# A two-batch encoder layer: eight places for the split operands of the seven block products, later stores of y, uneven output steps per attention round, and 30 steps ahead of the mixture

## Chip, core and metric

The kernel runs on one core of one Trainium2 chip. Its time is the device time of one execution in microseconds; several runs are shown and their median is compared. Beside them stands one execution under the hardware profiler, from which all durations here are read.

## What is computed

One hybrid encoder layer runs on two token sets with the same weights: A (`x_prompt`, 1024 tokens) and B (`x_sample`, 512 tokens), 1024 channels, all in float32.

```python
h = rms_norm(x, pre_w)
cols = jnp.einsum('bsd,dc->bsc', h, w_in)
y_m = mlstm_mixer(...) * jax.nn.silu(m_z)          # 1024 wide
y_a = dilated_attention(a_qkv, rel_table) * jax.nn.silu(a_z)   # 3 groups x 8 heads x 64
p_m = jnp.einsum('bsc,cd->bsd', y_m, w_pm)
p_a = jnp.einsum('bsc,cd->bsd', y_a, w_pa)
merged = g[:, :, 0] * p_m + g[:, :, 1] * p_a
out = jnp.einsum('bsd,de->bse', merged, w_out)
return x + rms_norm(out, post_w)
```

The three dilation groups of the attention are mixed with weights made of their row maxima and softmax denominators ("the mixture").

## The kernel before

**Arithmetic.** Float32 products are made of rounded halves: every operand is split into a high part (ScalarE copy) and a low part (VectorE subtraction), and `mm3` (L233 to L235) issues three matmuls: high x high, high x low, low x high. One such triple on 128x512 is one *step* of the filling work. The large products of A's output side (`w_proj_m` and `w_out` on 1024 x 1024 x 1024 pieces) are made with seven block products in place of eight (i = 0 to 6): sums and differences of the operand quadrants are formed on GpSimd (L2248), split into *places* by `divide` (L2233 and L2234), multiplied, and added up by VectorE when a PSUM bank is evicted.

**Order of the work.** TensorE and the SP queue run in the program's order; the other engines' instructions are placed by the framework's scheduler. `Fill` holds the filling work as a list of generators that give one step at a time. The mixers (mLSTM, attention, the mixture) are the foreground: after each of their rounds they call `fill(share)`, and `fill.stage(steps, shares)` sets how many steps a share is worth. When B's attention begins (L2877), 768 steps are done. What then follows, in steps: the last four input units (32); for A the projection `proj_m` in seven block products of 16 (112), `proj_a` (64) and `final`, the output product with the closing norm, again seven of 16 (112); then B's branches: `proj_m` (64), `proj_a` (32), and B's `final` (64). 1248 steps in all.

**B's attention** (`attend`, L1926) runs 12 heads' pairs x 4 tiles = 48 rounds and three closing ones. In the last 16 rounds (group 2, `compact`) four rounds form a batch: scores (`lg`, L1719), maxima and exponents (L1730, L1732 on VectorE, L1734 on ScalarE), two transposes (`pt`, L1742), and the output product (`o`, L1751). `STEPS[3] = 290` steps are spread over the 48 rounds, 6.04 each.

**The mixture** (`combine`, L2032) follows for B's four token tiles t. It loads the rows `og_b` that attention has stored (`V0a`, `V1a`), forms weights on VectorE (`weigh`, L2052 to L2062), scales (`mix`, L2069), adds (L2075), transposes on TensorE (`tp`, L2080) and multiplies with the gate (L2082). Its first load is issued at the first `next(mixed)`; two shares of filling follow before the first `weigh`, of 66/18 steps each times two.

**A's `final`** (L2391). Its operands a0, b0, a1, b1 are the four merged quadrants. `combined` (L2237) lists the splits and sums as jobs; a job that reuses a place is held until the last step that read it. The places are a ring: `V0b`, `V1b` and `H0` in `proj_m`, `V0b`, `V1b` and `K1` in `final`, two places each, so six. The evictions are L2431 to L2447: `u` (`H1`), `o` (`H2`), `x` (`H0`) hold running sums. When a token tile is complete, `square` sums squares on ScalarE (L2414) and multiplies with the norm's weight on GpSimd (L2415), and `close` adds it to the residual on VectorE (L2424) and queues the store of y. Queued stores of y go to the SP queue at the next eviction in `final` (`flush`), or after two ticks.

**B's `proj_m`** needs the eight rows `yb` of B's mLSTM output, split by `split` (L2152; L2167 on ScalarE, L2168 on VectorE) while the last 26 steps of `final` run: into `X0`, `K0` (rows 0 to 3) and `H3`, `H2` (rows 4 to 7). They come through three row buffers (`ymr`, `sraw`), whose loads stand in GpSimd's queue.

Of the kernel before, what the change touches and what calls it, by code (L numbers as in the profile page):

```python
# [29 lines left out]
P = 128  # L30
# [174 lines left out]
class Net:  # L205
# [1720 lines left out]
    def attend(self, T, fill, steps, first, banks, outs, after=None, beside=None, at=()):  # L1926
# [5 lines left out]
        with ExitStack() as st:  # L1932
# [269 lines left out]
    def outputs(self, T, before):  # L2202
# [34 lines left out]
        def combined(kind, ring, uses, begun):  # L2237
# [46 lines left out]
        def proj_m(weights):  # L2284
            ring = M["ring"] + slots("H0")
            M["a1"], M["b1"] = four("H1"), four("H2")
            quadrant(M["b1"], 4, 1)
            quadrant(M["a1"], 0, 1)
            for n in range(2):
                gate(n)  # L2290
            u, x = four("H3"), four("Q1")
            pm = M["pm"] = {(0, 0): four("X0"), (0, 1): u, (1, 1): x}
            uses = [(i, k) for i in range(7) for _ in range(4) for k in range(4)]
# [10 lines left out]
            def evict(i, p, ps):  # L2304
                q, r = u[:, p], x[:, p]
                if i == 0:
                    nc.scalar.activation(q, ps, AF.Copy)
                elif i in (1, 4):
                    if (i, p) == (4, 0):
                        pm[1, 0] = four("K0")  # L2310
                    y = pm[i // 4, 0][:, p]
# [21 lines left out]
            def halves(b, k):  # L2333
                if k == 0:
                    ya.append([four(z, F32R) for z in (("K1", "H1"), ("H2", "H0"))[b]])
# [4 lines left out]
            for b, t in ((0, 82), (1, 97)):  # L2340
                late += [(t + k, lambda b=b, k=k: row(b, k)) for k in range(3)]
# [49 lines left out]
        def final(weights):  # L2391
            fill, sb = weights.__self__, self.osb
            ring = M["ring"] + slots("K1")
            u, o, x = four("H1"), four("H2"), four("H0")
            tiles = [(i, t) for i in range(7) for t in range(4)]
# [21 lines left out]
            def close(b, t, ys):  # L2417
# [5 lines left out]
                for h, y in enumerate(ys):  # L2423
                    nc.vector.scalar_tensor_tensor(xt[h], y, s[:, 6:7], xt[h], op0=OP.mult, op1=OP.add)  # L2424
                    self.pending.append((self.clock + 2, "y", (T.y[r0:r0 + P, h * S:(h + 1) * S], xt[h]), ("xo", which)))

            def evict(i, t, ps):
                q, r = u[:, t], x[:, t]
                self.flush(lambda q: q[1] == "y")
                if i == 0:  # L2430
# [54 lines left out]
            assert not jobs  # L2485
            self.flush(lambda q: q[3] == ("xo", "gab"))
            self.xo_bufs = [q for q in self.xo_bufs if q[0] != "gab"]
            self.retired = self.spare_place
            free = len(self.wsplit) - (len(fill.ready) - fill.base)
            places = [self.take(z) for z in ("Q1", "H0")]  # L2490
            self.wsplit[free:free] = [[z[:, 1024 * i:1024 * (i + 1)] for i in range(2)] for z in places]
# [139 lines left out]
SHORT = 768  # L2631
STEPS = (316, 260, 192, 290, 66)


def body(tc, a):
# [3 lines left out]
    with ExitStack() as st:  # L2639
# [158 lines left out]
        with ExitStack() as s1:  # L2798
# [82 lines left out]
            with ExitStack() as s2:  # L2881
# [80 lines left out]
```

## Time and profile before

| what | value |
| --- | --- |
| time of the runs shown | 2222.4, 2214.58, 2217.93 us; median 2217.93 us |
| the profiled execution's own time | 2215.37 us |
| its span, first to last instruction | 2213.6 us |
| mean granted TensorE clock | 0.989 |
| TensorE matmuls | 2168.8 us busy, 98% of the span, 11530 instructions |
| VectorE | 1531.7 us, 69% |
| ScalarE | 1093.1 us, 49% |
| GpSimd | 850.5 us, 38% |
| DMA | 408.22 MB, mean 184 GB/s |

A row of the profile reads: line of the kernel, engine, operation, output tile <- input tiles, shape, count; then busy time and mean duration, then idle time of that engine just before, and what ended it. In a timeline the first two numbers are the start and the duration in us, and the bracket holds the idle time ahead. Matmuls overlap in the pipeline, so their starts tell the pace, not their durations. PEclk is the granted TensorE clock, 1.00 for full speed.

### The profile page before, as it was taken

How to read it: one execution, taken by the hardware profiler on the slowest of the kernel's cores; microseconds unless marked ns; L12 is line 12 of the kernel's file. 1: busy time of each engine (PE TensorE's matmuls, PEld its weight loads, DVE VectorE, ACT ScalarE, POOL GpSimd, SP SyncE). 2: the span in 40 equal slices, each digit the busy share in tenths (PEclk: the TensorE clock that was granted, in tenths of full speed). 3: DMA queues.
4: the chain of work that ended last, by engine and by line, in shares of the span. 5: the costliest groups of instructions: out<-in, count | busy, mean ns of one | idle time of the engine just before them, and what ended most of it. 6: DMA issues, size and time to landing. Idle time of an engine off the chain costs nothing. (4 is left out here: it accounts for less than half of the span.)

```text
span 2213.6 us, 33670 instructions
## 1 busy us (share of the span) xinstructions
PE 2168.8 (98%) x11530; PEld 1847.1 (83%) x11530; DVE 1531.7 (69%) x2967; ACT 1093.1 (49%) x2252; POOL 850.5 (38%) x1077
## 2 busy tenths in 40 slices
PE   9999999999999999999999999999999999999598
PEld 8988888888888888888888889998888878877487
DVE  8766565667778776548887765665578748857774
ACT  7322243344444433447776666666655545436322
POOL 1000432333335663236677630011155443475531
PEclk9999999999999999999999999999999999999799
DMA  3642454723335553386755658977687785745763
GB/s 137 191 137 79 149 163 143 220 105 114 105 114 179 181 197 134 118 271 216 237 166 179 194 176 240 280 205 199 210 279 260 243 285 155 233 136 173 257 203 112
DMA packets 213430, 408.22 MB, mean 184 GB/s; under 512 B 36905, under 2 KB 118505, under 8 KB 213258
## 3 DMA queue, kind: packets, MB, share of 16 engines
q1 hardware_dynamic: 184104, 298.17, 42.3%
q0 software_dynamic: 25552, 95.30, 13.4%
q10 hardware_dynamic: 3602, 12.59, 1.4%
q8 instruction: 91, 1.49, 0.3%
q14 instruction: 81, 0.66, 0.1%
HBM read 278.91 MB, written 127.07 MB: 183 GB/s over the span
## 5 line engine op out<-in xcount | busy, mean ns | idle before, releaser
L234 PE MATMUL dense<-H,wh 128*128 128x512 f32 x700 | 276.2, 395 | 5.8 <-DVE H L2168 5.8
L233 PE MATMUL dense<-H,wh 128*128 128x512 f32 x660 | 270.0, 409 | 11.7 <-ACT H L2167 11.7
L235 PE MATMUL dense<-H,wl 128*128 128x512 f32 x660 | 260.2, 394 | 0.0
L233 PE MATMUL d<-Hh,phla 128*128 128x512 f32 x608 | 236.5, 389 | 0.0
L235 PE MATMUL d<-Hh,phla 128*128 128x512 f32 x608 | 236.5, 389 | 0.0
L234 PE MATMUL d<-Hl,phla 128*128 128x512 f32 x608 | 236.5, 389 | 0.0
L302 DVE TENSOR_TENSOR wl<-wraw,wh 128x1024 fp32r<-128x1024 f32 (+1 forms) x122 | 153.9, 1263 | 41.1 <-ACT wh L296 40.8
L235 PE MATMUL d<-Hh,phlb 128*128 128x512 f32 x456 | 177.4, 389 | 0.0
L233 PE MATMUL d<-Hh,phlb 128*128 128x512 f32 x456 | 177.4, 389 | 0.0
L234 PE MATMUL d<-Hl,phlb 128*128 128x512 f32 x456 | 177.4, 389 | 0.0
L296 ACT ACTIVATE wh<-wraw 128x1024 fp32r<-128x1024 f32 (+1 forms) x125 | 129.3, 1036 | 61.7 <-PE dense L234 33.7
L234 PEld LDWEIGHTS dense<-H,wh 128*128 128x128 f32 x700 | 133.0, 190 | 22.7 <-DVE H L2168 6.7
L782 POOL TENSOR_TENSOR psum_w<-pw_raw 128x512 f32<-128x512 f32 x38 | 59.5, 1565 | 236.1 <-DMA pw_raw<-w_in 154.3
L233 PEld LDWEIGHTS dense<-H,wh 128*128 128x128 f32 x660 | 125.2, 190 | 29.1 <-ACT H L2167 12.9
L235 PEld LDWEIGHTS dense<-H,wl 128*128 128x128 f32 x660 | 124.8, 189 | 28.1
L1839 DVE CUSTOM_DVE_ANT_0 ls<-lg,bias 128x256 f32<-128x256 f32 (+2 forms) x240 | 78.7, 350 | 89.7 <-PE lg L1820 51.8
L234 PEld LDWEIGHTS d<-Hl,phla 128*128 128x128 f32 x608 | 114.1, 188 | 23.7
L233 PEld LDWEIGHTS d<-Hh,phla 128*128 128x128 f32 x608 | 114.1, 188 | 23.7
L819 POOL TENSOR_TENSOR psum_w<-pw_raw,psum_w 128x512 f32<-128x512 f32 x38 | 49.3, 1298 | 220.1 <-DVE phla L764 220.1
L235 PEld LDWEIGHTS d<-Hh,phla 128*128 128x128 f32 x608 | 114.1, 188 | 23.7
L1843 ACT ACTIVATE ls<-ls,nm 128x256 f32<-128x256 f32 (+1 forms) x192 | 87.3, 456 | 80.0 <-DVE nm L1841 49.2
L233 PE MATMUL d<-v,Hh 128*128 128x484 f32 (+1 forms) x336 | 121.3, 361 | 0.1
(780 smaller groups left out, 6011.7 us busy)
## 6 DMA issues: line engine op xcount, KB each, us to landing
pw_raw<-w_in SPq DMA_DIRECT2D x76, 512.0 KB, 3.8
wraw<-w_in SPq DMA_DIRECT2D x63, 512.0 KB, 4.7
aqk_a<-pwk SPq DMA_DIRECT2D x32, 512.0 KB, 7.1
Q<-aqk_a SPq DMA_DIRECT2D x20, 512.0 KB, 6.3
wraw<-w_v POOLq DMA_DIRECT2D x22, 430.0 KB, 6.2
aqk_b<-sw SPq DMA_DIRECT2D x36, 256.0 KB, 6.5
aqk_a<-pwk SPq DMA_DIRECT2D x32, 256.0 KB, 3.8
qk_a<-pwk SPq DMA_DIRECT2D x16, 512.0 KB, 2.6
```

The lines of the kernel that those rows point to most:

```text
L233: nc.tensor.matmul(out, lh, rh, start=start, stop=False, **kw)
L234: nc.tensor.matmul(out, lh, rl, start=False, stop=False, **kw)
L235: nc.tensor.matmul(out, ll, rh, start=False, stop=stop, **kw)
L296: high = nc.scalar.activation(hi[:, :n], raw[:, :n], AF.Copy)
L302: low = (self.lows or nc.vector).tensor_sub(lo[:, :n], raw[:, :n], hi[:, :n].bitcast(F32))
L782: self.nc.gpsimd.tensor_add(s[:, 0], ws[1][:, 0], ws[1][:, 1])
L819: nc.gpsimd.tensor_sub(s[:, 1], wa[:, 1], s[:, 1])
L1839: nc.vector.tensor_tensor_reduce(out=ls[rows, hh], in0=ts["lg"][hh][rows, of], in1=bt[rows, hh, by], scale=1.0, scalar=NEG, op0=OP.add, op ...
L1843: self.held = self.held[-3:] + [nc.scalar.activation(ls[:, hh], ls[:, hh], AF.Exp, bias=nm[:, hh:hh + 1], accum_out=ot[:, 128 + hh:129 + hh])]
```

## The change

Four things are changed together.

1. *Eight places.* The ring of `proj_m` becomes `V0b`, `V1b`, `H0`, `Q1`, that of `final` `V0b`, `V1b`, `K0`, `Q1`. To make room, the tile `x` is taken only when i = 3 begins (`H1` in `proj_m`, `H3` in `final`), b1 - a0 is written over a0 in place of a1, and the tiles are dealt out anew: B's rows `yb` go to `H1`, `K1` (rows 0 to 3) and `H2`, `K0` (rows 4 to 7), B's attention rows to `Q1`, `X0`.
2. *y a round later.* `final` no longer flushes the queued stores of y at each eviction; they wait for the next tick of the foreground. Two more buffer pairs for the residual are cut out of `X0`, when the tile (4, 3) asks for one.
3. *Uneven steps.* The first 32 rounds of B's attention get 6.5 steps each, the last 16 get 3. The number of steps done when attention ends falls from 308 (step 1076) to 265 (step 1033).
4. *Thirty steps ahead of the mixture.* The first four shares after attention, which lie between the first load of the mixture and its first `weigh`, are worth 30 steps in all; the other 14 shares 61.

The number of matmuls and of steps is the same (1248 steps in both). In the changed kernel lines up to L1967 are the same, and later ones lie 4 to 14 lines further down: L2168 becomes L2172, L2424 becomes L2431, L2415 becomes L2422.

```diff
-            fill.stage(steps, 12 * T.n)
-
-            self.xo_end = fill.done + steps
+            wide, narrow = steps if T.n <= 4 else (steps / (12 * T.n),) * 2
+            fill.stage(wide, 1)
+            rounds = 8 * T.n
+
+            self.xo_end = fill.done + 8 * T.n * wide + 4 * T.n * narrow
...
+                    if len(tiles) == rounds:
+                        fill.stage(narrow, 1)
...
-        return self.four((("X0", "K0", "H3", "H2"), ("V0b", "K1", "V1b", "H1"))[which][i], dt)
+        return self.four((("H1", "K1", "H2", "K0"), ("V0b", "Q1", "V1b", "X0"))[which][i], dt)
...
-            jobs += parts(3, a1) + sums(sub, a1, b1, a0)
-            jobs += parts(4, b0) + parts(5, a1) + parts(6, b1)
+            jobs += parts(3, a1) + sums(sub, a0, b1, a0)
+            jobs += parts(4, b0) + parts(5, a0) + parts(6, b1)
...
-            ring = M["ring"] + slots("H0")
+            ring = M["ring"] + slots("H0") + slots("Q1")
...
-            u, x = four("H3"), four("Q1")
-            pm = M["pm"] = {(0, 0): four("X0"), (0, 1): u, (1, 1): x}
+            u, x = four("H3"), None
+            pm = M["pm"] = {(0, 0): four("X0"), (0, 1): u}
...
+                if (i, p) == (3, 0):
+                    x = pm[1, 1] = four("H1")
...
-            ring = M["ring"] + slots("K1")
-            u, o, x = four("H1"), four("H2"), four("H0")
+            ring = M["ring"] + slots("K0") + slots("Q1")
+            u, o, x = four("H0"), four("H2"), None
...
-                    self.pending.append((self.clock + 2, "y", (T.y[r0:r0 + P, h * S:(h + 1) * S], xt[h]), ("xo", which)))
+                    self.pending.append((self.clock + 1, "y", (T.y[r0:r0 + P, h * S:(h + 1) * S], xt[h]), ("xo", which)))
...
-                self.flush(lambda q: q[1] == "y")
+                nonlocal x
+                if (i, t) == (3, 0):
+                    x = four("H3")
...
-                        M["o1"] = four("X0")
+                        M["o1"] = four("K1")
...
+                    if (i, t) == (4, 3):
+                        more = four("X0")
+                        self.xo_bufs[:0] = [(f"gab{j}", [more[:, 2 * j + k] for k in range(2)]) for j in range(2)]
...
-STEPS = (316, 260, 192, 290, 66)
+STEPS = (316, 260, 192, (6.5, 3), 30, 61)
...
-                fill.stage(STEPS[4], 3 * B.n + 6)
+                fill.stage(STEPS[4], 4)
                 fill(2)
                 next(mixed)
                 fill(2)
+                fill.stage(STEPS[5], 3 * B.n + 2)
```

On SP, at the end of B's attention, stands before (`og_b` is what attention has to store for the mixture, `V0a` the mixture's first load, `y_prompt` the stores of y):

```order
L249 DMA og_b<-sg 256x1x132 x2
L249 DMA y_prompt<-gab 128x512 x2
L249 DMA y_prompt<-bias_17605 128x512
L249 DMA y_prompt<-bias_17606 128x512
L249 DMA og_b<-ot 256x1x132 x2
L249 DMA y_prompt<-xo_17587 128x512
L249 DMA y_prompt<-xo_17588 128x512
L249 DMA y_prompt<-xo_17589 128x512
L249 DMA y_prompt<-xo_17590 128x512
L249 DMA y_prompt<-gab 128x512 x2
L249 DMA og_b<-sg 256x1x132 x2
L274 DMA V0a<-og_b 128x1584
```

and in the changed kernel:

```order
L249 DMA og_b<-sg 256x1x132 x2
L249 DMA og_b<-ot 256x1x132 x2
L249 DMA og_b<-sg 256x1x132 x2
L274 DMA V0a<-og_b 128x1584
L249 DMA y_prompt<-gab 128x512 x2
L249 DMA y_prompt<-xo_20060 128x512
L249 DMA y_prompt<-xo_20061 128x512
```

The ten stores of y that stood ahead of the last rows of `og_b` and of the mixture's first load now stand behind them.

On VectorE, at the last two splits that B's `proj_m` needs, stands before (`X_20341` is the mixture of tile t = 0, `H_20205` the low parts of rows 4 to 7 of `yb`, `wl`, `Q` and `H_20431` low parts of weights, L2524 the first eviction of B's `proj_m`):

```order
L2059 TENSOR_TENSOR wd_20458<-wd_20458 128x8
L2060 RECIPROCAL wd_20458<-wd_20458 128x8
L2062 SCALAR_TENSOR_TENSOR cw_20453<-cw_20453,wd_20458 128x24
L302 TENSOR_TENSOR Q_20430<-wraw_7243,Q_20430 128x1024
L2069 TENSOR_TENSOR X_20341<-V0a,cw_20453 128x512 x3
L2075 TENSOR_TENSOR X_20341<-X_20341 128x512 x2
L2168 TENSOR_TENSOR H_20205<-ymr_17586,H_20204 128x512
L2168 TENSOR_TENSOR H_20205<-sraw,H_20204 128x512
L302 TENSOR_TENSOR H_20431<-wraw_7244,H_20431 128x1024
L2524 SCALAR_TENSOR_TENSOR V0b<-gab,dense 128x512
```

and in the changed kernel (`X_20069` with `cw_20495` is the mixture of tile t = 2, `K_20248` the low parts of rows 4 to 7):

```order
L2066 SCALAR_TENSOR_TENSOR cw_20495<-cw_20495,wd_20500 128x24
L2073 TENSOR_TENSOR X_20069<-V0a,cw_20495 128x512 x3
L2431 SCALAR_TENSOR_TENSOR xo_20060<-H_19476,ss,xo_20060 128x512
L2431 SCALAR_TENSOR_TENSOR xo_20061<-H_20012,ss,xo_20061 128x512
L302 TENSOR_TENSOR wl_7248<-wraw_7244,wh_7247 128x1024
L2079 TENSOR_TENSOR X_20069<-X_20069 128x512
L302 TENSOR_TENSOR H_20478<-wraw_7243,H_20478 128x1024
L2172 TENSOR_TENSOR K_20248<-ymr_17586,H_20247 128x512
L2079 TENSOR_TENSOR X_20069<-X_20069 128x512
L2172 TENSOR_TENSOR K_20248<-sraw,H_20247 128x512
L2537 SCALAR_TENSOR_TENSOR V0b<-gab,dense 128x512
```

Before, the mixture of one tile stands ahead of these two splits; now those of three tiles (t = 0, 1, 2) do.

On VectorE, where the operands of the second block product of A's `proj_m` are split, stands before (`K_17627` is b0; `V0b` is a place that the first block product has used, `nm` and `ls` belong to the attention):

```order
L1839 ISA ls,ot<-lg,bias_17604 64x128
L1839 ISA ot 64x1
L1841 TENSOR_SCALAR nm<-ot 128x2
L2234 TENSOR_TENSOR V0b<-K_17627,V0b 128x512 x2
L2234 TENSOR_TENSOR V1b<-K_17626,V1b 128x512 x2
L1839 ISA ls,ot<-lg,bias_17605 128x256
```

and in the changed kernel, some 60 rows earlier, while the mLSTM's last products (`ym`) are formed:

```order
L302 TENSOR_TENSOR wl_7250<-wraw_7243,wh_7249 128x1024
L2238 TENSOR_TENSOR V1b<-K_17626,V1b 128x512 x2
L1545 TENSOR_TENSOR ym_7369<-a,X_15433 128x256
L302 TENSOR_TENSOR wl_7246<-wraw_7244,wh_7245 128x1024
L2238 TENSOR_TENSOR Q_17870<-K_17627,Q_17870 128x512 x2
L1839 ISA ls,ot<-lg,bias_17603 128x256
```

Two of the four splits of that product have moved to a place that nothing has used (`Q1`).

More of the change, by code (lines that the diff above doesn't have):

```diff
@@ L2304, in evict @@
             def evict(i, p, ps):
-                q, r = u[:, p], x[:, p]
+                nonlocal x
+                if (i, p) == (3, 0):
+                    x = pm[1, 1] = four("H1")
+                q, r = u[:, p], x is not None and x[:, p]
                 if i == 0:
@@ L2309, in evict @@
                     if (i, p) == (4, 0):
-                        pm[1, 0] = four("K0")
+                        pm[1, 0] = four("K1")
                     y = pm[i // 4, 0][:, p]
@@ L2334, in halves @@
                 if k == 0:
-                    ya.append([four(z, F32R) for z in (("K1", "H1"), ("H2", "H0"))[b]])
+                    ya.append([four(z, F32R) for z in (("K0", "H2"), ("Q1", "H0"))[b]])
                 hi, lo = ya[b]
@@ L2339, in proj_m @@
             late = []
-            for b, t in ((0, 82), (1, 97)):
+            for b, t in ((0, 84), (1, 96)):
                 late += [(t + k, lambda b=b, k=k: row(b, k)) for k in range(3)]
@@ L2485, in final @@
             assert not jobs
-            self.flush(lambda q: q[3] == ("xo", "gab"))
-            self.xo_bufs = [q for q in self.xo_bufs if q[0] != "gab"]
+            extra = [q[0] for q in self.xo_bufs if "gab" in str(q[0])]
+            self.flush(lambda q: q[3] is not None and q[3][0] == "xo" and q[3][1] in extra)
+            self.xo_bufs = [q for q in self.xo_bufs if q[0] not in extra]
             self.retired = self.spare_place
             free = len(self.wsplit) - (len(fill.ready) - fill.base)
-            places = [self.take(z) for z in ("Q1", "H0")]
+            places = [self.take(z) for z in ("H3", "H0")]
             self.wsplit[free:free] = [[z[:, 1024 * i:1024 * (i + 1)] for i in range(2)] for z in places]
```

3 lines of the change are left out of this document (2 added, 1 removed).

## Prediction

> **What bounds the kernel now.** The page's table of engines and its slices come first.
>
> ```profile
> PE 2168.8 (98%) x11530; PEld 1847.1 (83%) x11530; DVE 1531.7 (69%) x2967; ACT 1093.1 (49%) x2252; POOL 850.5 (38%) x1077
> PE   9999999999999999999999999999999999999598
> PEclk9999999999999999999999999999999999999799
> ```
>
> TensorE is busy throughout, except in slice 38, where the granted clock falls too. No matmul is taken away by this change, so it can only win or lose in the places where TensorE waits. The waits of TensorE, longest first:
>
> ```profile
> PE dense L233 <- ACT H L2167: 11.7, 2, 10.1
> PE dense L234 <- DVE H L2168: 5.8, 1, 5.8
> ...
> PE dense L234 <- DVE V0b L2234: 2.6, 1, 2.6
> PE dense L233 <- DVE H L2447: 2.4, 1, 2.4
> ```
>
> L2167 and L2168 split `yb` for B's `proj_m`; L2447 is an eviction in A's `final`, L2234 splits an operand of a block product. After a wait the clock stays halved for a while, so I read the loss of each place from the windows: idle time, plus busy time times (1 - PEclk).
>
> ```profile
> 1820.00:1840.00 20.00, 17.37 (x92) 14.58 (x91) 18.40 (x26) 8.71 (x22) 11.12 (x12) 0.91 0.41 122
> ...
> 1960.00:1980.00 20.00, 18.24 (x98) 14.84 (x96) 12.46 (x26) 6.12 (x21) 19.29 (x17) 1.00 0.42 120
> 1980.00:2000.00 20.00, 18.86 (x95) 15.24 (x96) 10.97 (x32) 10.99 (x26) 8.34 (x7) 0.83 0.24 67
> ...
> 2040.00:2050.00 10.00, 7.92 (x33) 5.48 (x31) 10.00 (x16) 5.88 (x22) 4.19 (x4) 1.00 0.39 132
> 2050.00:2060.00 10.00, 8.28 (x40) 6.47 (x42) 9.26 (x13) 4.54 (x10) 7.88 (x12) 0.83 0.85 288
> ...
> 2070.00:2080.00 10.00, 4.60 (x13) 2.62 (x12) 6.33 (x9) 2.30 (x5) 9.47 (x14) 0.79 0.95 285
> 2080.00:2090.00 10.00, 0.78 (x2) 0.05 (x1) 3.21 (x8) 1.93 (x3) 0.78 (x2) 0.50 0.96 319
> 2090.00:2100.00 10.00, 3.36 (x7) 2.37 (x8) 8.97 (x17) 2.40 (x4) 4.47 (x8) 0.50 0.80 289
> 2100.00:2110.00 10.00, 10.00 (x38) 8.01 (x38) 8.01 (x17) 2.34 (x3) 5.46 (x10) 0.84 0.75 259
> ```
>
> Columns: window, length, busy time of PE, PEld, DVE, ACT and POOL with their counts, PEclk. The four places:
> - W1, A's `proj_m` (1820 to 1840): 2.63 idle + 0.09 x 17.37 = 4.2 us.
> - W2, start of A's `final` (1960 to 2000): 1.76 + 1.14 idle + 0.17 x 18.86 = 6.1 us.
> - W3, the middle of `final` (2040 to 2060): 2.08 + 1.72 + 0.17 x 8.28 = 5.2 us.
> - W4, where B's `proj_m` begins (2070 to 2110): 5.40 + 9.22 + 6.64 idle, and 1.0 + 0.4 + 1.7 + 1.6 of slow clock = 26.0 us.
>
> Together 41.5 us: more than that the change cannot win by these waits.
>
> Why W4 is long stands in the chain that ended last and in the timelines of TensorE and VectorE:
>
> ```profile
> 2073.15 7.45 DMA og_b<-sg
> 2080.74 7.75 DMA V0a<-og_b
> ```
>
> ```profile
> 2068.71 0.39 PE L233 MATMUL dense<-X,wh 128*128 128x512 f32 x1
> ...
> 2069.39 0.39 PE L233 MATMUL dense<-X,wh 128*128 128x512 f32 x1
> ...
> 2090.87 0.80 PE L233 MATMUL dense<-H,wh 128*128 128x512 f32 x1 [10.10 <-ACT H L2167]
> 2097.43 0.80 PE L234 MATMUL dense<-H,wh 128*128 128x512 f32 x1 [5.76 <-DVE H L2168]
> ```
>
> ```profile
> 2088.51 0.17 DVE L2052 TENSOR_TENSOR cw<-V0a 128x8 f32<-128x8 f32 x1 [6.72 <-DMA V0a<-og_b]
> ...
> 2093.56 1.89 DVE L2069 TENSOR_TENSOR X<-V0a,cw 128x512 f32<-128x512 f32 x3
> 2095.36 1.41 DVE L2075 TENSOR_TENSOR X<-X 128x512 f32<-128x512 f32 x2
> 2096.69 0.69 DVE L2168 TENSOR_TENSOR H<-ymr,H 128x512 fp32r<-128x512 f32 x1
> ...
> 2097.90 1.22 DVE L302 TENSOR_TENSOR H<-wraw,H 128x1024 fp32r<-128x1024 f32 x1
> ```
>
> The last stores of `og_b` and the load of `V0a` take 15 us one after the other. VectorE's first `weigh` waits for that load, and the last splits of `yb` stand behind the mixture in VectorE's queue. TensorE makes the first step of `proj_m` at 2068.71 (call it T; a step is 0.68 us, 2069.39 - 2068.71) and needs the eighth row of `yb` seven steps later, at T + 5. It comes at about T + 29 (2096.69 + 2 x 0.69 - 2068.71). The cause is thus a DMA wait *ahead of* some ten microseconds of VectorE work.
>
> **Part by part.**
>
> *Eight places.* W1 is a short ring: the splits of the second product's last two operands wait until the first product has left `V0b`, and then they run beside GpSimd's sums:
>
> ```profile
> 1820.43 2.55 POOL L2248 TENSOR_TENSOR K<-K,H 128x512 f32<-128x512 f32 x2
> 1820.64 5.94 DVE L2234 TENSOR_TENSOR V0b<-K,V0b 128x512 fp32r<-128x512 f32 x2 [1.95 <-ACT V0b L2233]
> ...
> 1826.03 0.50 PE L234 MATMUL dense<-V0b,sw 128*128 128x512 f32 x1 [2.63 <-DVE V0b L2234]
> ```
>
> Two splits took 5.94 us there. In the changed kernel they are placed some 60 rows earlier, in `Q1`, ahead of the sums. Later products have their places a whole product (16 steps, 11 us) ahead in place of about 5 steps. What is late next is the third product, whose splits still meet the sums, but it starts 16 steps after. I take W1 as gone: -4.2 us; bounds 0 and -4.2. The new dealing of the tiles adds no instruction; the waits that it could add (`K1` as output tile and then for `yb`, `H3` as a weight place after the last close) lie in the stretch of W4 and are counted there.
>
> *Uneven steps.* W3 comes from attention's VectorE work (`softmax`) beside `final`'s splits, evictions and closes, with two PSUM banks. In the changed kernel attention ends at step 57 of `final`, not 100; what was W3 then runs without attention and with four banks. VectorE's rows from eviction (3, 3) to (6, 1) add up to some 24 us in 40 steps (27 us). W3 goes: -5.2 us; bounds 0 and -5.2. W2 is this:
>
> ```profile
> 1970.74 1.09 PE L1719 MATMUL lg<-V0a,Q 128*64 128x128 f32 x16
> 1974.23 4.39 DVE L1732 TENSOR_SCALAR nm<-st 128x2 f32<-128x2 f32 x3
> ...
> 1978.86 0.33 ACT L1734 ACTIVATE ls<-ls,nm 128x64 f32<-128x64 f32 x1
> 1980.51 1.06 ACT L2431 ACTIVATE H<-dense 128x512 f32<-128x512 f32 x2
> 1981.14 0.80 PE L233 MATMUL dense<-sw,V0b 128*128 128x512 f32 x1 [2.90 <-ACT H L2431]
> ```
>
> Three tiny `nm` took 4.39 us while GpSimd was forming `final`'s sums back to back; the exponents wait for them, and the eviction stands behind the exponents. The first batch of group 2 is put six steps further from the end of `proj_a` (scores at step 985, before at 979; `proj_a` ends at 976), so less of it meets the sums; the eviction now stands behind six exponents, not eight. I take two of the 6.1 us: -2 us; bounds +2 (TensorE now also waits at the transpose) and -6.1.
>
> The new price: between scores and the first transpose of a batch lie 6 steps (4.1 us) in place of 12 or 13 (8 us). Four exponents must be done by then. In the second batch of the profile that took:
>
> ```profile
> 1996.44 1.04 PE L1719 MATMUL lg<-V1a,Q 128*64 128x128 f32 x16
> ...
> 2000.47 0.33 ACT L1734 ACTIVATE ls<-ls,nm 128x64 f32<-128x64 f32 x1
> ```
>
> From the scores' end (1997.5) to the fourth exponent's end (2000.8): 3.3 us, so that cover is thin but there; where VectorE first has splits to do, it is exceeded. I allow +2 us over four batches; bounds 0 and +20 (below).
>
> *y later, thirty steps ahead.* SP no longer holds ten stores of y in front of `og_b` and `V0a`, and 30 steps (20 us) lie between the load and the first `weigh`, against 15 us of DMA. So the DMA wait goes. But it is not what then holds the splits. In the changed order the mixtures of *three* tiles stand ahead of the last split of `yb`. Between eviction (6, 1), which cannot run before T - 5.4, and that split VectorE has: ten closes, eight splits, two evictions, six adds and one product with the gate, 27 x 0.69; nine scalings, 3 x 1.89; four weight splits, 4 x 1.22; 23 small rows of 0.17. That is 18.6 + 5.7 + 4.9 + 3.9 = 33 us; in a full queue the rows start a little closer (1.33 us for the two adds above, not 1.41), say 32. So the last split ends at T - 5.4 + 32 = T + 27, before T + 29. GpSimd's products with the norm's weight run beside it:
>
> ```profile
> L2415 POOL TENSOR_TENSOR H<-H,postw 128x512 f32<-128x512 f32 x9 | 13.7, 1529 | 5.5 <-ACT mg L2414 5.5
> L2234 DVE TENSOR_TENSOR V1b<-Q,V1b 128x512 fp32r<-128x512 f32 x2 | 3.8, 1891 | 0.7 <-ACT V1b L2233 0.7
> L2234 DVE TENSOR_TENSOR K<-H,K 128x512 fp32r<-128x512 f32 x2 | 1.4, 680 | 0.0
> ```
>
> The same split is 0.68 us alone and 1.89 us where it meets them, 1.2 us more. Five such products fall into the stretch; with about half of them met I add 3 us: T + 30. The transpose of tile 0, now three steps *before* the end of `final`, waits within the same stretch. So W4 keeps its size: +0.5 us; bounds -6 (the rows at their closest, 29 us, no collision, a shorter slow spell) and +5. This is the step that decides the size of the forecast: the wait for a DMA is replaced by VectorE work that was hidden behind `proj_m` before.
>
> Sum: -4.2 - 5.2 - 2 + 2 + 0.5 = -8.9 us. Against the profiled execution's own 2215.4 us that is 2206.5; it lies 2.5 us under the median of the runs, 0.1%. I predict 2206 us.
>
> **The rivals.** About 0.3%, 6.6 us, is what a measurement of this kernel can tell from no change; faster means under 2211.3, slower over 2224.6.
>
> *More goes than I count* (0.22). W2 goes whole (4 us more), the short rounds cost nothing (2), and W4 falls to its lower bound (6): 2206 - 12 = 2194. For it: the DMA wait of 6.72 us and the row loads' waits are gone for certain. Against it: the VectorE rows are counted, not guessed.
>
> *The gain is used up in VectorE's backlog* (0.17). Every GpSimd product of the stretch holds VectorE for its whole length: 5 x 1.53 = 7.6 us in place of 3, and W2 comes back whole at the new place (2 us): 2206 + 4.6 + 2 = 2213; with VectorE 3 us late at (6, 1), 2216. No change that can be told. The three `nm` that took 4.39 us speak for it, most splits at 0.68 us in W4's own stretch against it. The Trainium skill, SBUF — State Buffer, "Who interferes with whom", says that a VectorE instruction with two SBUF inputs and a GpSimd instruction that reads SBUF exclude each other, the second waiting until the first is through; closes, splits, scalings and adds all have two SBUF inputs, so by that rule putting more of them beside `final` speaks against the change. The trace agrees where both queues are full (5.94 us for two splits).
>
> *Slower: the three-step rounds* (0.11). In the first batch of the profile the fourth exponent (the row at 1978.86) ended 7.4 us after the scores (1978.86 + 0.33 - 1970.74 - 1.09). If all four batches take that long, TensorE waits 7.4 - 4.1 = 3.3 us in each, and the slow clock behind a wait costs 1.6 us more, as in W1: 4 x 4.9 = 20 us, 18 more than I allow: 2224 and, with W2 at its upper bound (+2 in place of -2), 2228. It decides from 4.1 us on between scores and fourth exponent. Against it: the second batch took 3.3 us.
>
> My own case keeps 0.50, and its range is 2200 to 2212. The range over all reaches from 2190 (half of the first rival) to 2221 (all of the second). Faster: 0.44 of my own 0.50, 0.22, and 0.02 of the second: 0.68. Same: 0.06, and 0.15 of the second: 0.21. Slower: 0.11.
>
> **What would show it.** Right: no wait at L2238 in A's `proj_m`; no wait at L2456 in `final`; no VectorE wait for `V0a<-og_b`; TensorE still waiting some 20 us for L2171 and L2172 and for the first `tp`, with VectorE busy without a gap; short waits at `pt` L1742. Wrong: VectorE done with the last split before T + 20, waits at L1742 of more than 2 us each, or a new wait for a place (`K1`, `H3`, `Q1`) that I put at nothing.

## The result and the profile after

The changed kernel takes 2224.5 us (median of 9 runs, 2221.19 to 2225.59) against 2217.97 us of the kernel before (9 runs): a ratio of 1.0024, 95% interval 1.0014 to 1.0034, slower by 0.24%. The forecast was 2206 us, with a range of 2190 to 2221; it missed in sign. The profiled execution took 2224.6 us (its span is 2222.8), near its own median, where that of before had been 2.6 us under its median; so the two profiles differ by 9.2 us, the medians by 6.5.

The waits of TensorE in the changed kernel, longest first:

```profile
PE tp L2084 <- DVE wd L2064: 15.5, 1, 15.5
PE pt L1742 <- ACT ls L1734: 7.6, 8, 2.2
PE dense L233 <- ACT H L2171: 7.5, 2, 7.0
PE dense L233 <- DVE X L2319: 7.1, 1, 7.1
PE dense L234 <- DVE K L2172: 3.2, 3, 1.3
```

Gone, as forecast, are the wait of A's `proj_m` for a split, those of `final` for its evictions, and VectorE's wait for the mixture's load. In their place stand the mixture's first transpose (`tp`), the transposes of the short rounds (`pt`; one of the eight, of 1.1 us, is in A's attention), and an eviction in A's `proj_m` (L2319) that was no wait at all before. The windows give the loss of each place, counted as before (idle time, plus busy time times 1 - PEclk):

```profile
1515.00:1535.00 20.00, 18.90 (x136) 15.77 (x136) 8.04 (x52) 12.71 (x46) 1.07 (x2) 1.00 0.69 187
1820.00:1840.00 20.00, 12.86 (x72) 10.79 (x70) 18.20 (x20) 7.46 (x18) 18.51 (x15) 0.88 0.51 151
1840.00:1860.00 20.00, 20.00 (x99) 17.10 (x100) 17.79 (x40) 10.59 (x29) 6.54 (x11) 0.87 0.54 161
1980.00:2000.00 20.00, 18.12 (x109) 13.89 (x109) 16.72 (x33) 9.72 (x30) 15.61 (x13) 0.91 0.37 108
2000.00:2020.00 20.00, 15.80 (x87) 11.82 (x86) 15.51 (x55) 12.21 (x46) 6.69 (x6) 0.91 0.50 140
2020.00:2040.00 20.00, 19.59 (x123) 15.48 (x122) 11.49 (x35) 10.95 (x29) 3.71 (x7) 1.00 0.45 146
2070.00:2080.00 10.00, 1.25 (x6) 0.68 (x4) 9.88 (x17) 2.56 (x9) 9.59 (x13) 0.70 0.84 280
2080.00:2090.00 10.00, 3.23 (x10) 2.78 (x11) 9.93 (x19) 2.47 (x5) 5.87 (x8) 0.50 0.65 206
2090.00:2100.00 10.00, 6.43 (x22) 4.00 (x21) 9.71 (x17) 2.58 (x7) 4.80 (x5) 0.95 0.44 145
2100.00:2110.00 10.00, 2.79 (x6) 1.82 (x7) 8.80 (x16) 3.19 (x5) 4.22 (x8) 0.56 0.78 282
2110.00:2120.00 10.00, 10.00 (x44) 8.14 (x43) 6.20 (x15) 2.23 (x3) 2.60 (x5) 0.92 0.88 288
```

| place | before, us | forecast | after | how the number of after is made |
| --- | --- | --- | --- | --- |
| A's attention, 1515 to 1535 | 0 | 0 | 1.1 | 1.10 idle |
| W1, A's `proj_m` | 4.2 | 0 | 11.3 | 7.14 idle + 0.12 x 12.86 + 0.13 x 20 |
| W2 and W3, `final` beside attention, with the short rounds | 11.3 | 6.1 | 9.5 | 1.88 + 4.20 + 0.41 idle + 0.09 x (18.12 + 15.80) |
| W4, start of B's `proj_m` | 26.0 | 26.5 | 30.6 | 26.3 idle + 4.3 of slow clock |

Together +11.0 us; the spans differ by 9.2. The other 1.8 us are spread over the rest of the program and were not followed. The largest miss is W1. On VectorE stands there:

```profile
1831.37 7.77 DVE L2238 TENSOR_TENSOR V1b<-K,V1b 128x512 fp32r<-128x512 f32 x1
...
1839.13 0.67 DVE L2319 TENSOR_TENSOR X<-H,dense 128x512 f32<-128x512 f32 x1
```

and on GpSimd and TensorE in the same time:

```profile
1831.83 1.30 POOL L2252 TENSOR_TENSOR K<-K,K 128x512 f32<-128x512 f32 x1
1833.07 1.27 POOL L2252 TENSOR_TENSOR K<-H,K 128x512 f32<-128x512 f32 x1
1834.29 1.26 POOL L2252 TENSOR_TENSOR K<-K,K 128x512 f32<-128x512 f32 x1
1835.50 0.57 POOL L274 DMA_DIRECT2D gab<-gt_a  x1
1836.09 2.49 POOL L2252 TENSOR_TENSOR K<-H,K 128x512 f32<-128x512 f32 x2
```

```profile
1839.86 0.79 PE L233 MATMUL dense<-H,wh 128*128 128x512 f32 x1 [7.14 <-DVE X L2319]
```

One split took 7.77 us, eleven times the 0.68 us of the same split alone. It ended 0.6 us after the last of five GpSimd sums (1836.09 + 2.49 = 1838.58; 1831.37 + 7.77 = 1839.14). It was a split for the third product, whose place `V1b` TensorE did not read before 1848.41; but an eviction of the second product stood behind it in VectorE's queue, and TensorE waited 7.14 us for the PSUM bank.

In the kernel before, GpSimd's sums stop earlier:

```profile
1826.12 3.27 POOL L2248 TENSOR_TENSOR K<-K,K 128x512 f32<-128x512 f32 x2 [0.70 <-DVE V0b L2234]
```

With these two, which end at 1829.39, twelve of the sixteen are formed; the other four follow from 1844 on. The second product's first eviction starts in the gap between, at 1832.48. In the changed kernel fifteen are formed by 1838.58, three of the last four among them (`K<-H,K`), and the second product's first two evictions start at 1826.79 and 1839.13.

W4, from eviction (6, 1), which ran at 2070.76, to the end of the last split of `yb`:

```profile
2070.76:2109.15 38.39, 12.10 (x38) 7.96 (x36) 37.68 (x65) 10.04 (x20) 22.87 (x32) 0.68 0.67 226
```

```profile
2072.16 1.75 DVE L2431 SCALAR_TENSOR_TENSOR X<-K,ss,X 128x512 f32<-128x512 f32 x1
2073.84 1.38 DVE L2057 TENSOR_TENSOR cw<-cw,V1a 128x8 f32<-128x8 f32 x1
...
2075.22 1.57 DVE L2427 SCALAR_TENSOR_TENSOR ss<-ss 128x1 f32<-128x1 f32 x1
...
2077.32 1.75 DVE L2172 TENSOR_TENSOR K<-sraw,H 128x512 fp32r<-128x512 f32 x1
...
2084.18 1.76 DVE L2427 SCALAR_TENSOR_TENSOR ss<-ss 128x1 f32<-128x1 f32 x1
...
2093.93 1.26 DVE L2427 SCALAR_TENSOR_TENSOR ss<-ss 128x1 f32<-128x1 f32 x1
...
2108.47 0.68 DVE L2172 TENSOR_TENSOR K<-sraw,H 128x512 fp32r<-128x512 f32 x1
```

VectorE was busy for 37.68 of these 38.39 us: the backlog of the forecast, which had put the stretch at 35 us (32 of rows and 3 of collisions). The six longer rows alone took 7.4 us more than rows of their kind do undisturbed (0.74, 0.15, 0.15, 0.68, 0.15 and 0.15 us).

TensorE's wait of 7.0 us for L2171 has three things in front of it. The last two loads of `yb` stand in GpSimd's queue behind a power:

```profile
2095.27 1.56 POOL L2428 TENSOR_TENSOR ss<-ss,mhalf 128x1 f32<-128x1 f32 x1
2096.80 0.62 POOL L274 DMA_DIRECT2D ymr<-ym_b  x1
```

They land 3.8 and 4.3 us after their issue (2096.80 and 2097.41). But ScalarE splits the first of them only at 2105.52, behind a copy of weights that begins right when the last closes of `final` have ended (2103.07 + 1.41 = 2104.48):

```profile
2103.07 1.41 DVE L2431 SCALAR_TENSOR_TENSOR xo<-H,ss,xo 128x512 f32<-128x512 f32 x2
```

```profile
2104.56 1.06 ACT L296 ACTIVATE H<-wraw 128x1024 fp32r<-128x1024 f32 x1 [3.46 <-issue]
2105.52 0.61 ACT L2171 ACTIVATE H<-ymr 128x512 fp32r<-128x512 f32 x1
```

```profile
2106.19 0.80 PE L233 MATMUL dense<-H,wh 128*128 128x512 f32 x1 [7.00 <-ACT H L2171]
```

By the kernel's lines the copy writes a tile that these closes read: `x` of `final` is `H3` (L2437), and so is the first weight place behind `final` (L2503). In the kernel before that place was `Q1`, a line of the change that the diff above doesn't show. The profile names no wait for this copy; in the run postw_dve, below, it puts a wait of 4.88 us of the same copy down to the close. And VectorE, busy all the time, reaches the low part of that row at 2107.27 only, so that TensorE waits once more behind it (1.0 us at 2108.01).

### The profile page after: what moved, and what is told of

It is laid out like the page before. It is cut to its first block, busy times and chain, and to the rows that moved or that the text cites. A ratio compares the mean times of both kernels' runs of the same rounds, so it can differ in the third digit from the quotient of the medians.

```text
span 2222.8 us, 33653 instructions
## 1 busy us (share of the span) xinstructions
PE 2168.5 (98%) x11530; PEld 1847.0 (83%) x11530; DVE 1543.7 (69%) x2967; ACT 1091.7 (49%) x2252; POOL 856.0 (39%) x1077
## 4 chain that ended last, share of the span: by engine, by line
PE 89%; DVE 4%; issue 2%; ACT 2%; POOL 1%; DMA 1%; SPq 0%; DVEq 0%; POOLq 0%; ACTq 0%
PE d L235 14%; PE d L233 14%; PE d L234 14%; PE dense L233 11%; PE dense L234 11%; PE dense L235 11%; PE lg L1820 2%; PE pt L1850 1%; PE o L1893 1%; PE num L1513 1%; PE num L233 1%; PE num L234 1%; PE num L235 1%; PE o L1872 1%; PE a L1220 1%
## 5 line engine op out<-in xcount | busy, mean ns | idle before, releaser
L233 PE MATMUL dense<-H,wh 128*128 128x512 f32 x644 | 263.0, 408 | 14.7 <-ACT H L2171 7.5
L234 PE MATMUL dense<-H,wh 128*128 128x512 f32 x652 | 256.5, 393 | 0.0
L235 PE MATMUL dense<-H,wl 128*128 128x512 f32 x644 | 254.1, 395 | 0.0
L233 PEld LDWEIGHTS dense<-H,wh 128*128 128x128 f32 x644 | 122.5, 190 | 31.8 <-ACT H L2171 8.4
L234 PEld LDWEIGHTS dense<-H,wh 128*128 128x128 f32 x652 | 123.7, 190 | 14.4
```

The source lines that it names most:

```text
L233: nc.tensor.matmul(out, lh, rh, start=start, stop=False, **kw)
L234: nc.tensor.matmul(out, lh, rl, start=False, stop=False, **kw)
L235: nc.tensor.matmul(out, ll, rh, start=False, stop=stop, **kw)
```

## Experiments

Each was timed with the kernel before on the same chip; the ratio to it is compared with the changed kernel's 1.0024.

| run | what it is | median, us | ratio to before, 95% interval |
| --- | --- | --- | --- |
| ring6 | changed, six places in `proj_m` | 2223.77 | 1.0034 (1.0023 to 1.0046) |
| even15 | changed, steps as before | 2223.30 | 1.0031 (1.0018 to 1.0044) |
| sums_dve | changed, sums of `proj_m` on VectorE | 2217.11 | 1.0006 (0.9997 to 1.0015) |
| postw_dve | changed, norm's products on VectorE | 2207.26 | 0.9957 (0.9942 to 0.9972) |
| rows_sp | changed, loads of `yb` on SP | 2216.46 | 0.9997 (0.9989 to 1.0006) |
| both_dve | changed, both on VectorE | 2200.20 | 0.9924 (0.9911 to 0.9936) |
| both_52 | the same, 52 steps ahead | 2204.51 | 0.9940 (0.9924 to 0.9955) |
| clean | both_dve and rows_sp | 2205.60 | 0.9954 (0.9942 to 0.9967) |
| clean_dummy | clean and 16 products on GpSimd that nobody reads | 2214.06 | 0.9994 (0.9985 to 1.0003) |
| before_dve | before, both on VectorE | 2200.48 | 0.9922 (0.9910 to 0.9935) |
| before_rows | the same, loads of `yb` on SP | 2202.92 | 0.9938 (0.9926 to 0.9951) |
| before_all | before_dve, final's sums too | 2195.52 | 0.9904 (0.9889 to 0.9919) |
| after_all | changed, all three on VectorE | 2196.78 | 0.9907 (0.9892 to 0.9922) |
| after_all_ns | after_all, A's attention as before | 2194.74 | 0.9904 (0.9888 to 0.9921) |

### Undoing one part: the places, the steps

The theory was that the eight places had let the held split in (L, "lock"); its rival, that the pace of the attention rounds had (P).

```diff
-            ring = M["ring"] + slots("H0") + slots("Q1")
+            ring = M["ring"] + slots("H0")
```

> The changed kernel, but with six places again for the split operands of A's proj_m (the other parts of the change stay). The changed kernel's median is 2224.5 us, that of before 2218.0. Theory L (lock): the eight places let the splits of the third block product into VectorE's queue among GpSimd's sums; one of them takes 7.77 us, an eviction stands behind it, TensorE waits 7.14 us. With six places that wait is not over 3 us: about 7 us less, 2217.5 us, at most 2219. Rival P (pace): the 6.5 steps per attention round bring evictions and sums too close together, whatever the places are: a wait of 5 us or more stays in A's proj_m and the time is 2222 us or more.

```diff
-STEPS = (316, 260, 192, (6.5, 3), 30, 61)
+STEPS = (316, 260, 192, (290 / 48, 290 / 48), 44 / 3, 154 / 3)
```

> The changed kernel, but with 6.04 steps in each attention round and 14.7 steps ahead of the mixture, as before: only the eight places and the later stores of y are left of the change. Theory L (lock): the wait in A's proj_m stays, since it hangs on the places (about 11 us lost there, before 4.2); the waits at the two transposes of a batch in final are gone, the one at the mixture is that of before or less: 2223 us, not under 2220. Rival P (pace): with 6.04 steps the wait in A's proj_m is 3 us or less, and the time is that of before or less, 2218 us or under.

Neither gave the time back: 1.0034 and 1.0031. ring6 came out as P has it, even15 as L has it, so neither explains both. The wait for L2319 stayed in both. In ring6 (the wait, and the row of VectorE that ran ahead of it):

```profile
PE dense L233 <- DVE X L2319: 5.1, 1, 5.1
```

```profile
1828.89 6.04 DVE L1841 TENSOR_SCALAR nm<-ot 128x2 f32<-128x2 f32 x1
```

and in even15:

```profile
PE dense L233 <- DVE X L2319: 5.1, 3, 3.8
```

```profile
1823.77 8.45 DVE L2238 TENSOR_TENSOR V0b<-K,V0b 128x512 fp32r<-128x512 f32 x2 [1.95 <-ACT V0b L2237]
```

With six places it is a tiny `nm` (256 numbers) that was held for 6.04 us; with the steps of before two other splits, for 8.45 us. So it is no one row that the eight places let in, as the theory had it, and not the pace alone. In each of the three orders VectorE comes to a split or an `nm` while GpSimd forms sums, that row is held, and the eviction stands behind it.

### Taking GpSimd's products away

```diff
-            sub, add = nc.gpsimd.tensor_sub, nc.gpsimd.tensor_add
+            eng = nc.vector if kind == "m" else nc.gpsimd
+            sub, add = eng.tensor_sub, eng.tensor_add
```

> The changed kernel, but the 16 sums and differences of A's proj_m are formed on VectorE in place of GpSimd. Theory L (lock): a sum on GpSimd holds VectorE for about its whole length, 1.3 to 1.7 us, and on VectorE it takes 0.69 us, so VectorE gets work and yet is done sooner: no split over 1.5 us between 1815 and 1840, no wait over 3 us in A's proj_m, 2217 us (7 less than the changed kernel). Rival F (VectorE is full): 16 x 0.69 = 11 us more stand in front of the splits and the evictions, the wait of 7.1 us grows by about as much as is not hidden: 2226 to 2232 us.

```diff
-                nc.gpsimd.tensor_mul(y, y, pw[:, h * S:(h + 1) * S])
+                nc.vector.tensor_mul(y, y, pw[:, h * S:(h + 1) * S])
```

> The changed kernel, but final's products with the norm's weight are formed on VectorE in place of GpSimd. Theory L (lock): where B's proj_m begins, VectorE is busy without a gap, and its rows were held some 7 us by GpSimd (five products of 1.4 us, four tiny powers of 1.0 us); on VectorE the five products take 5 x 0.69 = 3.5 us, and the powers still hold it. The wait at the first transpose of the mixture (15.5 us) gets 2 to 4 us shorter: 2221.5 us. Rival F (VectorE is full): nothing is held, so 3.5 us are added there: 2228 us.

sums_dve came as theory L has it: VectorE's rows from 1815 to 1842 by line (minimum, median and maximum in ns)

```profile
L2238 DVE TENSOR_TENSOR V0b<-K,V0b x2: 682/684/686, 1818.9 to 1822.0; 128x512 fp32r<-128x512 f32 x2
L2238 DVE TENSOR_TENSOR V1b<-K,V1b x2: 684/684/684, 1825.5 to 1826.2; 128x512 fp32r<-128x512 f32 x2
```

show every split at 0.68 us, and W1's wait is 0.75 us. It is worth 0.0018, 4 us, where 7 were expected; that lies at the edge of what the two intervals, each about 0.001 to a side, hold. (Its profiled execution, 2212.88 us, was the fastest of its twelve, so the gain is read from the medians, not from the two profiles.) postw_dve gained far more than was expected, 0.0067 or 15 us against 2 to 4. Part of it is in VectorE's busy time, on the pages of the changed kernel and of postw_dve:

```profile
PE 2168.5 (98%) x11530; PEld 1847.0 (83%) x11530; DVE 1543.7 (69%) x2967; ACT 1091.7 (49%) x2252; POOL 856.0 (39%) x1077
```

```profile
PE 2163.5 (98%) x11530; PEld 1843.8 (84%) x11530; DVE 1535.9 (70%) x2983; ACT 1092.1 (50%) x2252; POOL 832.9 (38%) x1061
```

VectorE does 16 products more (16 x 0.69 = 11 us) and is busy for 7.8 us *less*: the 16 products on GpSimd had held it for some 19 us. The expectation had counted the stretch of W4 alone.

### GpSimd's queue or the lock

postw_dve takes two things away: the hold, and the products that stand ahead of the row loads in GpSimd's queue. The next run moves the loads and leaves the products.

```diff
-                        self.fetch(("ym", T.S, min(r // 2, 4)), t[:, :w], T.ym[r, :, b * BLK:b * BLK + w], self.side)
+                        self.fetch(("ym", T.S, min(r // 2, 4)), t[:, :w], T.ym[r, :, b * BLK:b * BLK + w],
+                                   nc.sync if row < 8 and T not in self.mixed else self.side)
```

> The changed kernel, but the loads of the eight rows yb for B's proj_m stand in SP's queue in place of GpSimd's; all products stay where they are. Forming the products with the norm's weight on VectorE had gained some 15 us against the changed kernel where a lock of VectorE was to explain 2 to 4. Theory Q (GpSimd's queue): the loads of the last rows of yb are issued at 2096.80 and 2097.41 behind the last such product and the last power, and TensorE then waits 7.0 us for their split (L2171); without the products in that queue the loads are early. Moved to SP the wait of 7.0 us and the slow clock behind it go: about 10 us less than the changed kernel (ratio to before near 0.998). Rival L (lock alone): the rows come earlier, but their splits stand in VectorE's queue behind the same held rows: within 2 us of the changed kernel (ratio 1.0015 to 1.0035).

```profile
PE dense L233 <- ACT H L2171: 1.6, 2, 1.2
```

The 7.0 us wait went, and 6 us with it (0.0027): more than the rival allows, less than the 10 of theory Q. But the edit moved more than the loads, for the framework placed the work of VectorE and ScalarE anew. In the changed kernel the last two splits of `yb` run on VectorE at 2107.27 and 2108.47, behind the third tile's mixture (its scaling at 2101.26); in rows_sp they run at 2098.58 and 2099.48, ahead of it (2101.15). On ScalarE they now run ahead of the copy into `H3` (2097.91 and 2098.51, the copy at 2099.73). So the 6 us are the worth of the loads and of this order together, and how much of it was GpSimd's queue is not shown. postw_dve, where the loads stayed in GpSimd's queue, has the last split ahead of the third tile's mixture too (2091.45, scaling at 2094.94), so its 15 us need not be the hold alone either.

The next pair adds products and takes nothing away: VectorE has the same instructions in both, nobody reads the additional products, and the row loads are in another queue.

> The changed kernel with the sums of A's proj_m and the products with the norm's weight on VectorE, and the loads of the eight rows yb in SP's queue. It is the base for the next run. The two on VectorE alone gave a ratio to before of 0.9924. If the row loads in GpSimd's queue still cost something there, 0.989 to 0.991; as that queue is nearly free of products, I expect no more than 2 us, 0.9915 to 0.9925.

```diff
                 nc.vector.tensor_mul(y, y, pw[:, h * S:(h + 1) * S])
+                nc.gpsimd.tensor_mul(junk, pw[:, h * S:(h + 1) * S], pw[:, h * S:(h + 1) * S])
```

> As the run clean, with 16 additional products on GpSimd whose results nobody reads (the norm's weight times itself, 128x512, into the scratch tile of the square), one behind each square in final. VectorE does the same work as in clean, the row loads stand in SP's queue. Theory L (lock): each such product holds VectorE for some 1.3 us if VectorE has work; six of them lie in the stretch in which VectorE has no gap, so the time is 8 us (5 to 12) over that of clean, 0.35% of the time, and VectorE's busy time rises by 10 us or more with the same instructions. Rival (no lock; the queue was all): within 2 us of clean, and VectorE's busy time stays.

The pages of clean and of clean_dummy:

```profile
PE 2160.5 (98%) x11530; PEld 1841.3 (83%) x11530; DVE 1531.8 (69%) x2999; ACT 1092.6 (50%) x2252; POOL 805.5 (37%) x1037
```

```profile
PE 2166.0 (98%) x11530; PEld 1844.3 (83%) x11530; DVE 1553.2 (70%) x2999; ACT 1092.6 (49%) x2252; POOL 825.0 (37%) x1053
```

8.5 us between the medians (2214.06 - 2205.60), where 8 were expected, and VectorE's busy time rises by 21.4 us with the same 2999 instructions: nearly the whole length of the 16 products (16 x 1.39 = 22.2 us). The busy time shows the hold by itself. The 8.5 us are less pure: the framework placed VectorE's rows in another order here too, and most of them do not lie where the expectation put them. The waits of W4 are the same in sum, 23.5 us in clean and 19.0 + 2.9 + 2.0 = 23.9 us in clean_dummy (the two smaller ones for L2171 and L2172); the longest of each:

```profile
PE tp L2084 <- DVE X L2079: 23.5, 1, 23.5
```

```profile
PE tp L2084 <- DVE wd L2064: 19.0, 1, 19.0
```

Counted in windows of 20 us, as above, the loss from 2060 to 2120 rises by 2.5 us only (27.4 to 29.9), and that beside attention's last rounds, from 1960 to 2060, by 5.2 us (5.2 to 10.4). That the sum came out near the 8 expected is in part luck.

clean itself missed its expectation, 0.9954 against 0.992: a load that SP issued at 2061.49 was used at 2070.68 only, VectorE idled 5 us behind it, and TensorE waited 23.5 us at `tp` in place of 16.5. So here the loads were better off in GpSimd's queue, once the products were gone from it.

### What the change is worth without the hold

> The kernel before, with the sums of A's proj_m and the products with the norm's weight on VectorE in place of GpSimd; nothing of the change. If GpSimd's work beside VectorE costs the kernel before as it costs the changed one (theory L): the waits of 2.6 us in proj_m and part of the 6 us at the start of final go, ratio 0.997 (6 us). If those costs come in by the change (its places and its three mixtures ahead of the splits): ratio 0.9990 to 1.002.

> The changed kernel with both, the sums of A's proj_m and the products with the norm's weight, on VectorE. The two lie in places that do not touch (around 1830 and from 1970 on), so the gains add: 4 to 5 us and 15 us off the changed kernel, ratio to before 0.9935 to 0.995. If it is 0.996 or more, they are not two costs but one.

> The kernel before, with all sums (of A's proj_m and of final) and the products with the norm's weight on VectorE; it had 0.9922 with final's sums still on GpSimd. Theory L: at the start of final the three tiny nm that GpSimd's sums held for 4.39 us come at once, the 2.9 us wait of TensorE there and its slow clock go: 4 to 6 us more, ratio 0.990. Rival F (VectorE is full): 11 us of sums stand between attention's rows, waits of TensorE at pt and at the evictions grow: 0.9925 or more.

> The changed kernel with all sums (of A's proj_m and of final) and the products with the norm's weight on VectorE, the counterpart of before_all (ratio 0.9904). If the change is worth nothing once GpSimd's products no longer hold VectorE (theory B, VectorE's rows are the same in both orders): 0.9895 to 0.9915. If the change's own gains (W2 and W3, the load ahead of the mixture) only show without the lock: 0.987 or less. If the short rounds and the early mixture cost where VectorE has 11 us more to do: 0.993 or more.

The edits are those of sums_dve and postw_dve, and for the last two `nc.vector` for all sums; the tiny powers stay on GpSimd. before_dve came out at 0.9922, far below the 0.997 expected, and both_dve at 0.9924, somewhat below its 0.9935; before_all and after_all at 0.9904 and 0.9907. With the same products moved, the kernel before and the changed one cannot be told apart, in both pairs. With its sums and products on VectorE the kernel before has no wait in W1 with its six places (a window of before_all, PE busy 20.00 of 20):

```profile
1820.00:1840.00 20.00, 20.00 (x118) 17.60 (x117) 18.70 (x47) 12.54 (x33) 3.60 (x7) 1.00 0.54 167
```

nor one at the start of `final`. What both keep is W4: the longest waits of before_all, and then of after_all,

```profile
PE dense L233 <- ACT X L2167: 7.0, 1, 7.0
PE dense L233 <- ACT H L2167: 4.9, 1, 4.9
```

```profile
PE tp L2084 <- DVE X L2079: 16.5, 1, 16.5
```

with 2.0 and 1.9 us more for splits in before_all: 15.8 us in one order, 16.5 in the other. before_all is the fastest kernel of these but for what cannot be told from it, 0.96% below before (interval 0.81 to 1.11%).

### Moving W4

> As the kernel with both on VectorE, and 52 steps ahead of the mixture in place of 30 (39 for the rest): TensorE meets the mixture's first transpose some 20 steps later, after B's proj_m has begun. Theory B (VectorE's backlog): the wait of 15 to 16 us at that transpose goes, but as VectorE has no gap there, part of it comes back as waits for the splits of yb: 6 to 10 us less than with 30 steps, ratio near 0.991. Rival 1: it all comes back, no gain. Rival 2: it goes whole, 17 us or more less.

> The kernel before, with the sums of A's proj_m and the products with the norm's weight on VectorE (0.9922) and the loads of the rows yb in SP's queue. There, SP's queue holds ten stores of y and the mixture's load before; the waits at B's proj_m add up to 14.3 us. If the rows were late by GpSimd's queue: 3 to 6 us less, 0.990. If VectorE's backlog holds their splits (theory B): within 2 us, 0.9915 to 0.993; SP's queue could also make them later: 0.994 or more.

```diff
-STEPS = (316, 260, 192, (6.5, 3), 30, 61)
+STEPS = (316, 260, 192, (6.5, 3), 52, 39)
```

With 52 steps the `tp` is passed without a wait, and the waits are back at the splits of `yb`:

```profile
PE dense L233 <- ACT H L2171: 9.6, 2, 5.5
...
PE dense L234 <- DVE K L2172: 4.8, 3, 2.6
```

9.6 + 4.8 = 14.4 us for the 16.5: rival 1, it all comes back, and the ratio, 0.9940, is no better than that of 30 steps. before_rows, at 0.9938, is slower than before_dve, or the same at best: taking the row loads out of GpSimd's queue gained nothing there.

### The wait in A's attention

```diff
-                    if len(tiles) == rounds:
+                    if len(tiles) == rounds and T.n <= 4:
```

> As after_all, but the second call of the filler's stage, which the change makes at the last third of each attention, is made in B's attention only. In A's attention that call sets the number of steps due back to the whole number done, so that one step and its neighbours change places there; all profiles with the change show a TensorE wait of 1.1 us at a pt of A's attention near 1527 us that no profile of before shows. Theory S: with the call left out that wait is gone, and the time is 1 to 1.5 us less (0.0005, less than this comparison can tell). Rival: the wait stays.

The wait of 1.1 us near 1527 us, present in the eleven other profiles with the change, is gone in this one; the difference in time, 0.0003, tells nothing, as foreseen. So it came from the second `fill.stage`, which drops the fraction of a step that was due.

## Why the prediction was wrong

- **W1, forecast gone, became 11.3 us.** This is the step that failed: "What is late next is the third product, whose splits still meet the sums, but it starts 16 steps after." The splits of the third product were indeed not wanted; but VectorE runs its queue in order, and they stood ahead of an eviction that was. The bounds of 0 and -4.2 left this out. And the cause of W1 was not a short ring: sums_dve removes the wait with eight places, before_all with six. The old order has the same hold (5.94 us for its two splits) and lost only 4.2 us there: by its trace the sums paused at 1829.39, before the second product's first eviction, so none stood behind a held row. Which part of the change lets three more sums into that run was not settled; undoing the places or the steps, one at a time, left the wait.
- **W2 and W3, forecast -5.2 in sum, gave -1.8.** That they would go with the attention's VectorE work was right for W3 (no idle time from 2040 to 2070). The price of the short rounds was mis-sized: seven waits of 6.5 us in all and their slow clock in place of 2.
- **W4, forecast +0.5, gave +4.6.** The mechanism was right: the DMA wait is gone, VectorE has no gap, the loss keeps its size. both_52, before_all and after_all show the same backlog in three orders, 14.4 to 16.5 us of waits. The collisions were mis-sized, 7.4 us in place of 3, which is the price of the second rival. That "the row loads' waits are gone for certain" was wrong: a wait of 7.0 us came up for the split of a late row, and 6 us went with it in rows_sp, by the loads and the new order together. In front of that split stood the copy into `H3`, one of the three places that the prediction put at nothing; what that copy costs by itself is not shown, for VectorE's backlog held the row's low part longer still.
- **A's attention, not in the sum, gave +1.1.** The text said that lines up to L1967 were unchanged, but A's attention runs the changed lines behind them too.
- **The rivals.** "The gain is used up in VectorE's backlog" named the mechanism that decided, for W4 and W2; it gave 2213 to 2216 because it wasn't carried to W1, where GpSimd is as busy and an eviction stands in the same queue. The rule that spoke against the change (the Trainium skill, SBUF — State Buffer, "Who interferes with whom") deserved more than 0.17: the 5.94 us for two splits in the trace of before were already its price, and were read as a short ring.

## What to carry to other kernels

A row of VectorE that takes many times its usual length beside GpSimd work is the thing to remove, before any reordering: here a product on GpSimd cost VectorE 1.3 us (21.4 / 16) and on VectorE 0.69, and moving 48 products and sums gained 0.96%, where rearranging places, stores and steps gained nothing. An edit that only moves work between queues can also change the order that the framework gives the other engines, so compare the order of the rows before a gain is put down to the edit. What isn't urgent may still be harmful: ask what stands behind it in its engine's queue. And where an engine is busy without a gap ahead of a wait, an earlier load or a later consumer only moves the wait; the backlog itself must shrink.

## What the runs showed of the hardware

- The hold isn't shared out between instructions: with five GpSimd sums of 1.25 to 1.30 us in a row, the one VectorE row got in only after the last (7.77 us), although GpSimd issued a DMA for 0.57 us between them. Rows of one or a few elements are held as long as large ones: the 128x1 row of L2427, eight times in the changed kernel, took 146 ns at least and 1761 at most. The hold shows as the length of the VectorE row, so it counts as busy time and not as a wait.

```profile
L2427 DVE SCALAR_TENSOR_TENSOR ss<-ss x8: 146/590/1761, 2046.3 to 2093.9; 128x1 f32<-128x1 f32 x8
```

- Evictions, which take one operand from PSUM, are not held: in the same kernel, from 1960 to 2110 us, twelve of them take 677 ns each on average, and 687 at most.

```profile
L2456 DVE TENSOR_TENSOR H<-H,dense 128x512 f32<-128x512 f32 x12 | 8.1, 677 | 3.5 <-PE dense L235 3.5
```

The Trainium skill, SBUF — State Buffer, "Who interferes with whom", states that a VectorE instruction with at most one SBUF input does not contend with GpSimd outside of certain modes, which `tensor_scalar`, the operation of `nm`, can enter. The trace agrees for these evictions, and the `nm` of 6.04 us is in keeping with it.
